# Pinning two engines to program order in a hybrid attention and RWKV-7 layer, with some side work issued in smaller lots

## The chip, the cores and the metric

The kernel runs on one core of one Trainium2 chip. A core has five engines with queues of their own: TensorE (PE, matmuls into PSUM), VectorE (DVE), ScalarE (ACT), GpSimd (POOL) and SyncE (SP, which here issues the transfers). They run side by side and wait for each other by semaphores. The metric is the device time of the core in microseconds (us); lower is better.

## The reference

One layer over 256 frames of width 4096, in float32. A combined projection feeds 16 heads of forgetting attention ("fox", 128 wide), 32 heads of RWKV-7 (64 wide) and a gate; the gated outputs go through an output projection and a layer norm with residual.

```python
proj = jnp.einsum('bsd,dc->bsc', x, w_in)
...
log_f = jax.nn.log_sigmoid(ff.astype(f32) + f_bias.astype(f32))
fox_out = _fox_attention(q, k, v, log_f)   # softmax(q.k/sqrt(Dh) + cumsum(log_f)[t] - cumsum(log_f)[s]), causal
...
rw = rw + (rw_prev - rw) * mu_shift        # token shift by one frame
w_raw = -jax.nn.softplus(-(w0 + jnp.tanh(wd) @ w_up)) - 0.5
decay = jnp.exp(-jnp.exp(w_raw)); a = jax.nn.sigmoid(a0 + ad @ a_up)
...
y = _rwkv7_scan(r, decay, k, v, -kk, kk * a)   # S_t = S_{t-1} diag(decay) + (S_{t-1} a) b^T + v k^T ; y_t = S_t r_t
y = groupnorm_per_head(y) * gn_gain + gn_bias + bonus
h = jnp.concatenate([fox_out, rwkv_out], axis=-1) * jax.nn.silu(z)
out = jnp.einsum('bsc,cd->bsd', h, w_out)
x = layernorm(ALPHA * x + out, ln_gain, ln_bias)
```

(Two calls and the group norm are written in short here.)

## The kernel before

**Weight pieces.** Both projections are long rows of matmuls whose weights stream from memory. A *piece* is two k-tiles by 512 columns, 512 KB: SyncE loads it (L220, four raw buffers), ScalarE casts it to the matmul's format as the high part (L141, four buffers), VectorE subtracts to get the low part (L142, three buffers), and TensorE runs 12 products with 512 columns each: for two k-tiles and two halves of the frames, high by high, high by the input's low part, and low by high (L147, L148, L149; in the output projection L880, L881, L882). There are 624 pieces beside the first block. They are called w{n}_{b}_{q}, with n the pair of heads (0 to 7), b the block of columns within it (0 to 3) and q the piece (0 to 15), then wo{b}_{q} for the output projection. The profile leaves the numbers n and b out, so w_7l is the low part of piece 7 of some block. The first block, with the small columns of the low-rank paths beside it, is loaded in another form (wl, wr). `weights()` keeps three split pieces in hand, so the split of piece q+2 is emitted before the products of piece q.

**Side work.** All else is written as Python generators that stand in `sides`. `slot()` takes one step of each; it is called twice in each piece, so one step is half a piece. `yield from wait(k)` lets k steps pass. The generators are:

- `ahead()`: `lora()` (L313 to L326, transposes and token shift of the low-rank columns, a Tanh), then `prepare(i)` for the 16 column tiles (decays, keys, norms; `front(i)`, L422 to L450, makes decay and rate).
- `chain()`: `forget()` (L337 to L360: the log sigmoid of the forget gate with an Exp and a Ln on ScalarE, a reciprocal L347, a scan L353, and transposes L359), then `rwkv(n)` for the eight pairs: masks (L553 and L561), a triangular inverse (L600, L603), centring of the values (L620 to L627), four chunks of state (L647, L678, L687 and the copies L650, L681, L693), the readout yp (L707, L709), and the group norm: square and gain L714, L716, sums over heads L457, L459 and L462, root L719 to L721, spreading L466, scaling L725 and L726.
- `unload(n, b, ...)`: takes a finished block's tile bk (copied out of PSUM by L918 or L920), transposes it on VectorE (L809), stores and reloads it by way of DRAM (L283: bt, raw), and shifts tokens (L277, L278) or makes silu (L371, L372).
- `fox(i)`: scores (L743, L744), mask, maximum, exponential, reciprocal and scaling (L750 to L754), transposes (L758, copied by L760) and the product with the values (L764, L765).
- `gate()`: silu times output and its split (L380, L383, L384), and a store (hd, reloaded as h for the output projection).

**PSUM.** Blocks accumulate in pairs of tiles from a pool of three (`pp`); the side work has five more (`ps`). So the second accumulator of a block can be written only after L920 has copied the first one of the block before.

**The output projection.** Its blocks run b = 0 and 1 interleaved, then 2 to 7. At the end of block 0 the work pool is closed and `load_tok(0)` and `load_tok(1)` are called: they load the residual and the rows of gain and bias (rr, one buffer, L866 and L867), and split these rows (L869, L871, L872). After each block, `add` (L891, L892) and `gain` (L896, L899, L900) bring it into the residual.

**Order.** The kernel is written with Tile: the program emits instructions, and a scheduler orders each engine's queue by its own model, subject to the data. `tc.keep_in_program_order(...)` fixes an instruction's place among the others so marked on its engine. Before, only a few are marked: the transfers issued through `issue()` (L283), the input's casts, and some transposes and copies; `behind()` holds two other groups behind the latest split:

```python
def behind(first):
    return tc.issue_after(latest[0].ins) if first else nullcontext()
```

Of the kernel before, what the change touches and what calls it, by code (L numbers as in the profile page):

```python
# [14 lines left out]
ALU = mybir.AluOpType  # L15
# [69 lines left out]
def layer(ctx: ExitStack, tc: tile.TileContext, xt, xtok, w_main, w_lora, w_first, muv, w_o, up, par, mulora, fbias, lng, lnb, cst, out):  # L85
    nc = tc.nc
    PS = bass.MemoryType.PSUM
# [36 lines left out]
    nc.vector.memset(warm, 0.0)  # L124
    tc.keep_in_program_order(nc.scalar.activation(warm, warm, AF.Tanh))
# [10 lines left out]
    latest = [None]  # L136

    def split(src, n, name, pool=wpool, tag="", cols=1024):
        hi = pool.tile([P, cols], F32R, tag="wh" + tag, name=name + "h", bufs=4 if pool is wpool else 1)
        lo = pool.tile([P, cols], F32R, tag="wl" + tag, name=name + "l")  # L140
        nc.scalar.copy(hi[:, :n], src[:, :n])  # L141
        latest[0] = nc.vector.tensor_tensor(lo[:, :n], src[:, :n], hi[:, :n].bitcast(F32), ALU.subtract)  # L142
        return hi, lo
# [14 lines left out]
    for n, (k0, k1) in enumerate(pieces):  # L158
        for k in range(k0, k1):
            t = xpool.tile([P, 2, S], F32R, tag=f"x{k}", name=f"x{k}")  # L160
            r = x_raw[n][:, (k - k0) * S : (k - k0 + 1) * S]
            tc.keep_in_program_order(nc.scalar.copy(t[:, 0, :], r))
            nc.vector.tensor_tensor(t[:, 1, :], r, t[:, 0, :].bitcast(F32), ALU.subtract)
# [10 lines left out]
    nc.vector.tensor_scalar(half, prm[:, 0:2, :], 0.5, None, ALU.mult)  # L174
    nkk = const.tile([P, G], F32, name="nkk")
    nc.vector.tensor_scalar(nkk, prm[:, PAR.index("k_k"), :], -1.0, None, ALU.mult)
    omm = const.tile([P, 3, G], F32, name="omm")
    nc.vector.tensor_scalar(omm, prm[:, 7:10, :], -1.0, 1.0, ALU.mult, ALU.add)
    oml = const.tile([LORA, 2], F32, name="oml")
    nc.vector.tensor_scalar(oml, mul, -1.0, 1.0, ALU.mult, ALU.add)  # L180
    ika = PAR.index("k_a")
    hka = const.tile([P, 2, G], F32, name="hka")
    nc.vector.tensor_scalar(hka[:, 0, :], prm[:, ika, :], 0.5, None, ALU.mult)
    nc.vector.tensor_scalar(hka[:, 1, :], prm[:, ika, :], -0.5, 1.0, ALU.mult, ALU.add)
    gneps = const.tile([P, 1], F32, name="gneps")
    nc.vector.memset(gneps, GN_EPS)

    def behind(first):
        return tc.issue_after(latest[0].ins) if first else nullcontext()
# [33 lines left out]
    def fetch():  # L223
        while len(raws) < 3 and stream:
            load()
        if raws:
# [7 lines left out]
            for j in range(2):  # L234
                r = raw[:, j * OB : (j + 1) * OB]
                nc.scalar.copy(hl[j], r)
                nc.vector.tensor_tensor(hl[2 + j], r, hl[j].bitcast(F32), ALU.subtract)
# [38 lines left out]
    def lerp(p, mu, om, dst):  # L276
        nc.scalar.mul(dst, p, om)  # L277
        nc.vector.scalar_tensor_tensor(dst[:, 1:], p[:, : S - 1], mu, dst[:, 1:], ALU.mult, ALU.add)  # L278
# [3 lines left out]
    def issue(out, src):  # L282
        tc.keep_in_program_order(nc.sync.dma_start(out=out, in_=src))  # L283
# [19 lines left out]
    for m in range(2):  # L303
        nc.scalar.copy(lw[:, m, :], acc_l[m][:, :LW])
        nc.scalar.copy(bk_0[:, m, :P], acc_l[m][:, LW:LA])
    ff = []

    def lora():
# [9 lines left out]
        nc.vector.tensor_scalar(u, fft[:NF, :S], fb, None, ALU.add)  # L318
        ff.append(u)
        for j in range(2):  # L320
            t = rp.tile([LORA, S], F32, tag="zt", name=f"lw{j}")
            lerp(lt2[:LORA, j * S : (j + 1) * S], mul[:, j : j + 1], oml[:, j : j + 1], t)
            if j == 0:
                nc.scalar.activation(t, t, AF.Tanh)
            nc.scalar.copy(lr[:, j, 0, :], t)
            nc.vector.tensor_tensor(lr[:, j, 1, :], t, lr[:, j, 0, :].bitcast(F32), ALU.subtract)  # L326
# [4 lines left out]
    def forget():  # L331
# [5 lines left out]
        nc.vector.tensor_scalar(e, u, -1.0, None, ALU.mult)  # L337
        nc.vector.tensor_tensor(e, e, u, ALU.min)
        nc.scalar.activation(e, e, AF.Exp)
        e1 = ft("fe1")  # L340
        nc.vector.tensor_scalar(e1, e, 1.0, None, ALU.add)
        lg = ft("flg")
        nc.scalar.activation(lg, e1, AF.Ln)
        rest = ft("frest")
        nc.vector.tensor_scalar(rest, e1, -1.0, None, ALU.add)
        nc.vector.tensor_tensor(rest, e, rest, ALU.subtract)
        nc.vector.reciprocal(e1, e1)  # L347
        nc.vector.tensor_tensor(rest, rest, e1, ALU.mult)
        nc.vector.tensor_tensor(lg, lg, rest, ALU.add)
        nc.vector.tensor_scalar(u, u, 0.0, None, ALU.min)  # L350
        nc.vector.tensor_tensor(lg, u, lg, ALU.subtract)
        nc.vector.memset(e, 1.0)
        nc.vector.tensor_tensor_scan(rest, e, lg, 0.0, ALU.mult, ALU.add)  # L353
        nc.vector.tensor_scalar(lg, rest, -1.0, None, ALU.mult)
# [5 lines left out]
        nc.vector.tensor_copy(ct, ctp[:, : 2 * NF])  # L360
# [8 lines left out]
    def silu2(z, key):  # L369
        th = t256("zt", key + "t")  # L370
        nc.scalar.activation(th, z, AF.Tanh, scale=0.5)  # L371
        nc.vector.scalar_tensor_tensor(z, th, 1.0, z, ALU.add, ALU.mult)  # L372
        szs[key] = z

    def gate(y, key, k):
# [4 lines left out]
        nc.vector.scalar_tensor_tensor(h, y, 0.5, szs[key], ALU.mult, ALU.mult)  # L380
        pool, tag, bufs = (rp, "hl", 2) if far else (xpool, f"x{k}", 1)
        hl = pool.tile([P, 2, S], F32R, tag=tag, name=f"hl{k}", bufs=bufs)
        nc.scalar.copy(hl[:, 0, :], h)  # L383
        nc.vector.tensor_tensor(hl[:, 1, :], h, hl[:, 0, :].bitcast(F32), ALU.subtract)  # L384
# [34 lines left out]
    def front(i):  # L419
        upt = ups[i]  # L420
        uph = rp.tile([LORA, 2, P], F32R, tag="uph", name=f"uph{i}")
        nc.scalar.copy(flat(uph), flat(upt))  # L422
        upl = rp.tile([LORA, 2, P], F32R, tag="upl", name=f"upl{i}")
        nc.vector.tensor_tensor(flat(upl), flat(upt), flat(uph).bitcast(F32), ALU.subtract)
# [9 lines left out]
        nc.scalar.activation(tw, lp[:, :S], AF.Tanh, scale=0.5, bias=half[:, 0, i : i + 1])  # L434
        ta = rt(f"ta{i}")
        nc.scalar.activation(ta, lp[:, S:], AF.Tanh, scale=0.5, bias=half[:, 1, i : i + 1])
        yield
        nc.vector.tensor_scalar(tw, tw, -0.5 * DECAY, -0.5 * DECAY, ALU.mult, ALU.add)
        L = rt(f"L{i}")
        nc.vector.tensor_tensor_scan(L, cs[:, C_SCAN : C_SCAN + S], tw, 0.0, ALU.mult, ALU.add)  # L440
        eL = rp.tile([P, NCH, C + 1], F32, tag="eL", name=f"eL{i}")
        nc.gpsimd.memset(eL[:, :, 0:1], 1.0)
        nc.scalar.activation(eL[:, :, 1:], ch(L), AF.Exp)
# [674 lines left out]
```

## Time and profile before

| | |
|---|---|
| median of three runs | 1937.24 us (1934.83 to 1940.58) |
| the profiled execution | 1935.4 us |
| its span in the trace | 1933.6 us |
| granted TensorE clock | 0.999 |
| VectorE busy | 1363.2 us |
| ScalarE busy | 963.5 us, with 18 loads of function tables |
| transfers | 420.04 MB, 217 GB/s on average |

A row of the timeline gives start and duration in us, engine, line, operation, the tiles written and read with their shapes, and in brackets how long the engine had been idle before and what ended that. A row of the waits gives the engine and the line that waited, whom it waited for, and then the total in us, how often, and the longest.

### The profile page before, as it was taken

What the parts mean: (1) busy time and instruction counts of PE and PEld (TensorE: products, weight loads), DVE (VectorE), ACT (ScalarE), POOL (GpSimd) and SP (SyncE); (2) the same over time, 40 slices, a digit from 0 to 9 for tenths busy, and PEclk for the clock granted to TensorE, in tenths of its full rate; (3) what the DMA queues carried; (4) which work ended last, traced back from release to release, by engine and by line L of the source; (5) the groups of instructions that cost most, each with busy time, mean ns of one, the idle gap of its engine ahead of it and who ended that gap; (6) DMA issues with size and microseconds to landing.
All of it is one profiled execution on the core that took longest, in us unless ns stands there. A gap on an engine that the chain in (4) does not pass through costs nothing.

```text
span 1933.6 us, 27829 instructions
## 1 busy us (share of the span) xinstructions
PE 1916.5 (99%) x9897; PEld 1594.4 (82%) x9897; DVE 1363.2 (71%) x2323; ACT 963.5 (50%) x1447; POOL 124.2 (6%) x207
## 2 busy tenths in 40 slices
PE   9999999999999999999999999999999999999998
PEld 9888788788888888888888888888888888888886
DVE  6677768857786778677857795779577856755555
ACT  6554464455545644464456444645464554443332
POOL 0020002000200020002000200020001001000000
PEclk9999999999999999999999999999999999999999
DMA  9577667767686778677867677777777777766564
GB/s 343 152 237 229 200 199 215 223 201 216 206 238 198 214 214 236 195 216 211 233 195 220 211 228 202 217 212 220 215 210 221 238 278 242 251 199 197 186 204 166
DMA packets 269391, 420.04 MB, mean 217 GB/s; under 512 B 142338, under 2 KB 169364, under 8 KB 269252
## 3 DMA queue, kind: packets, MB, share of 16 engines
q1 hardware_dynamic: 268820, 417.58, 70.7%
q8 instruction: 77, 1.26, 0.3%
q10 hardware_dynamic: 432, 0.69, 0.1%
q14 instruction: 62, 0.51, 0.1%
HBM read 388.55 MB, written 29.64 MB: 216 GB/s over the span
## 4 chain that ended last, share of the span: by engine, by line
PE 95%; DVE 3%; DMA 1%; issue 0%; ACT 0%; SPq 0%; DVEq 0%; ACTq 0%
PE acc L147 23%; PE acc L149 23%; PE acc L148 23%; PE oacc L880 6%; PE oacc L881 6%; PE oacc L882 6%; PE gp L536 1%; PE rh L647 1%; PE up L678 1%; PE sp L687 1%; PE accl L149 0%; PE accl L148 0%; PE accl L147 0%; PE yp L709 0%; DVE prod L600 0%; DVE xc L603 0%
## 5 line engine op out<-in xcount | busy, mean ns | idle before, releaser
L603 DVE TENSOR_REDUCE xc<-prod 128x8 f32<-128x16 f32 (+30 forms) x248 | 73.1, 295 | 6.5
L600 DVE TENSOR_TENSOR prod<-Nb,xc 128x8 f32<-128x8 f32 (+30 forms) x248 | 71.4, 288 | 6.5 <-DMA Nb<-nd 0.4
L142 DVE TENSOR_TENSOR w_6l<-w,w_6h 128x1024 fp32r<-128x1024 f32 x31 | 37.9, 1222 | 37.5 <-ACT w_6h L141 25.4
L142 DVE TENSOR_TENSOR w_5l<-w,w_5h 128x1024 fp32r<-128x1024 f32 x31 | 41.3, 1333 | 29.5 <-PE acc L149 23.2
L142 DVE TENSOR_TENSOR w_12l<-w,w_12h 128x1024 fp32r<-128x1024 f32 x31 | 38.0, 1227 | 33.5 <-issue 13.8
L740 POOL TENSOR_SCALAR_AFFINE_SELECT nb<-nb 128x128 f32<-128x128 f32 x32 | 15.8, 498 | 705.2 <-DMA nb<-ncd 514.0
L141 ACT CAST w_12h<-w 128x1024 fp32r<-128x1024 f32 x31 | 32.5, 1050 | 48.4 <-DMA w<-in_w_main_dram 19.1
L142 DVE TENSOR_TENSOR w_10l<-w,w_10h 128x1024 fp32r<-128x1024 f32 x31 | 37.9, 1223 | 24.0 <-issue 17.9
L142 DVE TENSOR_TENSOR w_7l<-w,w_7h 128x1024 fp32r<-128x1024 f32 x31 | 37.9, 1222 | 22.1 <-PE acc L149 15.3
L141 ACT CAST w_13h<-w 128x1024 fp32r<-128x1024 f32 x31 | 32.5, 1049 | 40.7 <-PE acc L148 29.0
L141 ACT CAST w_5h<-w 128x1024 fp32r<-128x1024 f32 x31 | 32.6, 1051 | 40.1 <-PE acc L148 37.1
L142 DVE TENSOR_TENSOR w_11l<-w,w_11h 128x1024 fp32r<-128x1024 f32 x31 | 37.9, 1221 | 19.7 <-PE acc L149 19.7
L142 DVE TENSOR_TENSOR w_8l<-w,w_8h 128x1024 fp32r<-128x1024 f32 x31 | 37.8, 1219 | 19.7 <-PE acc L149 15.4
L149 PE MATMUL acc<-w_7l,x 128*128 128x512 f32 x124 | 47.7, 394 | 3.9 <-DVE w_7l L142 3.8
L147 PE MATMUL acc<-w_8h,x 128*128 128x512 f32 x124 | 50.8, 410 | 0.0
L147 PE MATMUL acc<-w_7h,x 128*128 128x512 f32 x124 | 49.9, 403 | 0.2 <-ACT w_7h L141 0.2
L142 DVE TENSOR_TENSOR w_13l<-w,w_13h 128x1024 fp32r<-128x1024 f32 x31 | 37.9, 1222 | 17.2 <-issue 8.3
L147 PE MATMUL acc<-w_3h,x 128*128 128x512 f32 x124 | 49.9, 403 | 0.0
L147 PE MATMUL acc<-w_5h,x 128*128 128x512 f32 x124 | 49.8, 402 | 0.0
L147 PE MATMUL acc<-w_11h,x 128*128 128x512 f32 x124 | 49.8, 402 | 0.0
L147 PE MATMUL acc<-w_15h,x 128*128 128x512 f32 x124 | 49.6, 400 | 0.0
L147 PE MATMUL acc<-w_9h,x 128*128 128x512 f32 x124 | 49.2, 397 | 0.0
(813 smaller groups left out, 6518.7 us busy)
## 6 DMA issues: line engine op xcount, KB each, us to landing
w<-in_w_main_dram SPq DMA_DIRECT2D x496, 512.0 KB, 3.9
wo<-in_w_o_dram SPq DMA_DIRECT2D x128, 512.0 KB, 4.4
bt<-bk SPq DMA_DIRECT2D x88, 128.0 KB, 4.2
Nb<-nd SPq DMA_DIRECT2D x16, 512.0 KB, 4.7
hd<-hl SPq DMA_DIRECT2D x29, 256.0 KB, 3.5
h<-hd SPq DMA_DIRECT2D x29, 256.0 KB, 6.5
wr<-in_w_first_dram SPq DMA_DIRECT2D x15, 384.0 KB, 6.4
lr<-in_w_lora_dram SPq DMA_DIRECT2D x14, 336.0 KB, 5.2
```

The lines of the kernel that those rows point to most:

```text
L141: nc.scalar.copy(hi[:, :n], src[:, :n])
L142: latest[0] = nc.vector.tensor_tensor(lo[:, :n], src[:, :n], hi[:, :n].bitcast(F32), ALU.subtract)
L147: nc.tensor.matmul(acc[:, :n], xs[k][:, 0, tt], hi[:, o : o + n], start=(k == 0), stop=False)
L148: nc.tensor.matmul(acc[:, :n], xs[k][:, 1, tt], hi[:, o : o + n], start=False, stop=False)
L149: nc.tensor.matmul(acc[:, :n], xs[k][:, 0, tt], lo[:, o : o + n], start=False, stop=(k == KT - 1))
L536: nc.tensor.matmul(o, BK[h, u, c, :], lt[j][h, u, c], start=True, stop=True)
L600: first = nc.vector.tensor_tensor(prod[:, :, :, s + 1 :], nb[:, :, s : s + 1, s + 1 :].to_broadcast([P, 2, NJ, w]), xc[:, :, :, s + 1 :], ...
L603: nc.vector.tensor_reduce(xc[:, :, :, s : s + 1], prod[:, :, :, s:], AX.X, ALU.add)
L647: nc.tensor.matmul(rh[:, u * P : (u + 1) * P], LT[:, u, c, 0:P], flat(SVt[:, u, c]), start=True, stop=True)
L880: nc.tensor.matmul(acc, ht[k][:, 0, tt], hi, start=(k == 0), stop=False)
L881: nc.tensor.matmul(acc, ht[k][:, 1, tt], hi, start=False, stop=False)
L882: nc.tensor.matmul(acc, ht[k][:, 0, tt], lo, start=False, stop=(k == KT - 1))
```

## The change

Every instruction on VectorE and on ScalarE is marked to keep program order (`pin`). `latest`, `behind()` and the import of `nullcontext` go. TensorE, SyncE and GpSimd keep the marks they had. Further `yield`s split lots of side work in two, half a piece apart: after each half of the masks, after each half of the centring (the wait behind it is shorter by two), between the exponentials of the softmax and its scaling (the wait behind it is shorter by one), between the root and the reciprocal of the group norm, after each token shift, and between the two silus.

In the changed program as built, counts of instructions by engine stay the same, and so does the number of table loads; three of those at L371 move to L434 and three to L752.

```diff
+    pin = tc.keep_in_program_order
...
-    latest = [None]
-
     def split(src, n, name, pool=wpool, tag="", cols=1024):
         hi = pool.tile([P, cols], F32R, tag="wh" + tag, name=name + "h", bufs=4 if pool is wpool else 1)
         lo = pool.tile([P, cols], F32R, tag="wl" + tag, name=name + "l")
-        nc.scalar.copy(hi[:, :n], src[:, :n])
-        latest[0] = nc.vector.tensor_tensor(lo[:, :n], src[:, :n], hi[:, :n].bitcast(F32), ALU.subtract)
+        pin(nc.scalar.copy(hi[:, :n], src[:, :n]))
+        pin(nc.vector.tensor_tensor(lo[:, :n], src[:, :n], hi[:, :n].bitcast(F32), ALU.subtract))
         return hi, lo
...
-    def behind(first):
-        return tc.issue_after(latest[0].ins) if first else nullcontext()
...
     def forget():
...
-        nc.vector.tensor_scalar(e, u, -1.0, None, ALU.mult)
-        nc.vector.tensor_tensor(e, e, u, ALU.min)
-        nc.scalar.activation(e, e, AF.Exp)
+        pin(nc.vector.tensor_scalar(e, u, -1.0, None, ALU.mult))
+        pin(nc.vector.tensor_tensor(e, e, u, ALU.min))
+        pin(nc.scalar.activation(e, e, AF.Exp))
...
         for u in range(2):
             for j in range(2):
                 h = HALF[j]
-                nc.vector.tensor_tensor(gb[j][h, u], gv[u][j][h], m(h), ALU.mult)
+                pin(nc.vector.tensor_tensor(gb[j][h, u], gv[u][j][h], m(h), ALU.mult))
...
+            yield
         for u in range(2):
             for j in range(2):
                 o = HALF[1 - j]
-                nc.vector.tensor_tensor(lt[j][o, u], ..., ALU.mult)
+                pin(nc.vector.tensor_tensor(lt[j][o, u], ..., ALU.mult))
+            yield
...
                 for a in range(2):
-                    with behind(not n):
-                        nc.vector.scalar_tensor_tensor(SV[j][o, :, 2 * a + c, :], ...)
-            tc.keep_in_program_order(nc.scalar.copy(UV[j][o], SV[j][o]))
+                    pin(nc.vector.scalar_tensor_tensor(SV[j][o, :, 2 * a + c, :], ...))
+            pin(nc.scalar.copy(UV[j][o], SV[j][o]))
             nc.gpsimd.memset(SV[j][HALF[j], :, 0, :], 0.0)
-        yield from wait(W["d2"] - 1)
+            yield
+        yield from wait(W["d2"] - 3)
...
-        nc.vector.tensor_tensor(hr[:, 0, :], hr[:, 0, :], hr[:, 1, :], ALU.add)
-        nc.scalar.activation(hr[:, 0, :], hr[:, 0, :], AF.Sqrt, scale=1.0 / HD, bias=gneps)
-        nc.vector.reciprocal(hr[:, 1, :], hr[:, 0, :])
+        pin(nc.vector.tensor_tensor(hr[:, 0, :], hr[:, 0, :], hr[:, 1, :], ALU.add))
+        pin(nc.scalar.activation(hr[:, 0, :], hr[:, 0, :], AF.Sqrt, scale=1.0 / HD, bias=gneps))
+        yield
+        pin(nc.vector.reciprocal(hr[:, 1, :], hr[:, 0, :]))
         spread(flat(sd), hr[:, 1, :])
...
-        for m, blk in enumerate((slice(0, 1), slice(1, 3))):
-            with behind(i < 2):
-                nc.vector.scalar_tensor_tensor(lg[:, blk, :], spv[:, blk, :], ..., nb[:, blk, :], ALU.add, ALU.add)
-            nc.vector.tensor_reduce(st[:, m : m + 1], lg[:, blk, :], AX.XY, ALU.max, negate=True)
-            nc.scalar.activation(lg[:, blk, :], lg[:, blk, :], AF.Exp, ...)
-            nc.vector.reciprocal(st[:, 4 + m : 5 + m], st[:, 2 + m : 3 + m])
-            nc.vector.tensor_scalar(lg[:, blk, :], lg[:, blk, :], st[:, 4 + m : 5 + m], None, ALU.mult)
-        yield from wait(W["fp"])
+        blocks = list(enumerate((slice(0, 1), slice(1, 3))))
+        for m, blk in blocks:
+            pin(nc.vector.scalar_tensor_tensor(lg[:, blk, :], spv[:, blk, :], ..., nb[:, blk, :], ALU.add, ALU.add))
+            pin(nc.vector.tensor_reduce(st[:, m : m + 1], lg[:, blk, :], AX.XY, ALU.max, negate=True))
+            pin(nc.scalar.activation(lg[:, blk, :], lg[:, blk, :], AF.Exp, ...))
+        yield
+        for m, blk in blocks:
+            pin(nc.vector.reciprocal(st[:, 4 + m : 5 + m], st[:, 2 + m : 3 + m]))
+            pin(nc.vector.tensor_scalar(lg[:, blk, :], lg[:, blk, :], st[:, 4 + m : 5 + m], None, ALU.mult))
+        yield from wait(W["fp"] - 1)
...
                     rk[i, j] = shifted(raw[:, j, :], j, i)
+                    yield
...
         silu2(zf, f"f{i}")
+        yield
         silu2(zr, f"r{i}")
...
         rh = rpool.tile([6, OB], F32R, tag="rh", name=f"rh{b}")
-        nc.scalar.copy(rh, rr)
+        pin(nc.scalar.copy(rh, rr))
...
-        nc.vector.tensor_tensor(res[m][:, o], res[m][:, o], lgain[b], ALU.mult)
+        pin(nc.vector.tensor_tensor(res[m][:, o], res[m][:, o], lgain[b], ALU.mult))
         if m and b < HALVED:
             gx[b] = [rpool.tile([P, OB], F32R, name=f"g{'hl'[j]}{b}") for j in range(2)]
-            nc.scalar.copy(gx[b][0], res[m][:, o])
-            nc.vector.tensor_tensor(gx[b][1], res[m][:, o], gx[b][0].bitcast(F32), ALU.subtract)
+            pin(nc.scalar.copy(gx[b][0], res[m][:, o]))
+            pin(nc.vector.tensor_tensor(gx[b][1], res[m][:, o], gx[b][0].bitcast(F32), ALU.subtract))
```

Every other instruction of the two engines, here and in the parts left out, is wrapped in `pin(...)` in the same way and is otherwise unchanged.

More of the change, by code (lines that the diff above doesn't have):

```diff
@@ L1 @@
 import math
-from contextlib import ExitStack, nullcontext
+from contextlib import ExitStack
 import numpy as np
@@ L317, in lora @@
         u = rp.tile([NF, S], F32, tag="t", name="fu", bufs=5)
-        nc.vector.tensor_scalar(u, fft[:NF, :S], fb, None, ALU.add)
+        pin(nc.vector.tensor_scalar(u, fft[:NF, :S], fb, None, ALU.add))
         ff.append(u)
@@ L766, in fox @@
         o = t256("fq", f"fo{i}")
-        nc.scalar.copy(o, op[:, :S])
+        pin(nc.scalar.copy(o, op[:, :S]))
         while f"f{i}" not in szs or 2 * i >= FAR and not closed:
@@ L836, in unload @@
                 for t in range(2):
-                    nc.scalar.copy(pair[t], tr[:, t * S : (t + 1) * S])
+                    pin(nc.scalar.copy(pair[t], tr[:, t * S : (t + 1) * S]))
                 yield
@@ L845, in unload @@
             yield from wait(LAND - 1)
[L846 removed]
+        pin(nc.scalar.mul(fq, fq, FOX_SCALE))
         side(fox(i, fq, fk, vt))
@@ L933, in layer @@
                 for m in range(2):
-                    nc.scalar.copy(vt[:, m, :], acc[m][:, 2 * P :])
+                    pin(nc.scalar.copy(vt[:, m, :], acc[m][:, 2 * P :]))
             if b != 1:
@@ L1021, in row @@
         t = rpool.tile([P, P], F32R, name="l" + name)
-        nc.scalar.copy(t, zp[:, :P])
+        pin(nc.scalar.copy(t, zp[:, :P]))
         return t
@@ L1032, in finish @@
         nc.tensor.matmul(wp, l, rows[:, o], start=True, stop=True)
-        nc.vector.scalar_tensor_tensor(res[m][:, o], res[m][:, o], rss[m], wp, ALU.mult, ALU.add)
+        pin(nc.vector.scalar_tensor_tensor(res[m][:, o], res[m][:, o], rss[m], wp, ALU.mult, ALU.add))
     z0, _, last = moments(0)
```

233 lines of the change are left out of this document (116 added, 117 removed).

## The prediction

> **What bounds the kernel now.** I read the page's busy shares first, then the waits of TensorE, then the timelines of the stretches where the printed order of instructions, built from the changed program, differs most.
>
> ```profile
> span 1933.6 us, 27829 instructions
> ...
> PE 1916.5 (99%) x9897; PEld 1594.4 (82%) x9897; DVE 1363.2 (71%) x2323; ACT 963.5 (50%) x1447; POOL 124.2 (6%) x207
> ```
>
> TensorE is busy for 99% of the span, VectorE and ScalarE for 71% and 50%. So TensorE's queue sets the end, and the other two matter where they hand a split weight piece over late.
>
> ```profile
> PE acc L149 <- DVE w_7l L142: 3.8, 2, 3.4
> PE zp L1020 <- DVE zd L1008: 1.4, 1, 1.4
> PE warmup L108 <- POOL idle L105: 1.3, 1, 1.3
> ```
>
> These are the three largest of twelve rows. All twelve come to 10.1 us: that is everything a change on VectorE and ScalarE can win, and the second (the tail) and the third (the start) don't depend on it. The first row has the one long wait, of 3.44 us:
>
> ```profile
> 379.96 0.50 PE L149 MATMUL acc<-w_7l,x 128*128 128x512 f32 x1 [3.44 <-DVE w_7l L142]
> ...
> 380.00:383.00 3.00, 3.00 (x13) 2.46 (x14) 2.00 (x4) 1.59 (x3) 0.00 (x0) 1.00 0.65 199
> ```
>
> TensorE stood still until VectorE delivered the low part of a piece, and then ran on at a granted clock of 1.00, 13 products in 3.00 us or 0.23 us each. A piece has 12 products, so 2.73 us. Two pieces stand ready behind the one in use, so a hold-up of up to about 5.4 us on VectorE or ScalarE costs nothing, and each microsecond beyond it is a microsecond of the span.
>
> **The change part by part.** The instructions are the same ones; no product, cast or transfer is added. Three things move. The pins fix both engines' queues to the order in which the program emits work. The extra yields put parts of a lot half a piece later. And what the scheduler had pulled forward or spread out (the constants of the output, the forget gate, the group norm's end) falls back to where it is emitted. What that costs is read along the changed order, each instruction with its duration in the rows. For each signal between engines I add 0.05 and for each small product 0.1 (estimates from the gaps in the timelines).
>
> *First weight block.*
>
> ```profile
> 69.07 0.33 PE L149 MATMUL acc<-wr16l,x 128*128 128x384 f32 x1
> 69.25 0.39 PE L147 MATMUL acc<-w_0h,x 128*128 128x512 f32 x1
> ...
> 70.22 0.48 ACT L918 COPY bk<-acc 128x384 f32<-128x384 f32 x1
> ...
> 71.98 1.05 ACT L141 CAST w_4h<-w 128x1024 fp32r<-128x1024 f32 x1 [0.98 <-PE acc L148]
> ...
> 1655.11 1.22 DVE L142 TENSOR_TENSOR wo_0l<-wo,wo_0h 128x1024 fp32r<-128x1024 f32 x1
> ```
>
> Before, the three first casts of block w0_1 were made long ahead, and its first product starts 0.18 us after the last of the block before it. In the changed order both L918 copies stand ahead of the cast of w0_1_0, and the second waits for the last product, which ends at 69.40. Then 0.48 of copy and 1.05 of cast give 70.9, and 1.22 of subtraction gives 72.2. TensorE can do four products from the high part first, so the low part is due at 70.2: 2.0 us late. Six small transposes run inside the gap; I take 1.5.
>
> *Forget gate and low-rank path.*
>
> ```profile
> 74.23 0.47 DVE L318 TENSOR_SCALAR fu<-fft,fb 16x256 f32<-16x256 f32 x1 [0.80 <-PE fft L316]
> ...
> 80.32 1.73 DVE L347 RECIPROCAL fe<-fe 16x256 f32<-16x256 f32 x1
> ...
> 86.39 0.15 DVE L360 COPY ct<-ctp 128x32 f32<-128x32 f32 x1
> ...
> L809 DVE STREAM_TRANSPOSE bk<-bk x44: 690/702/716, 69.0 to 1419.3; 128x512 f32<-128x512 f32 x44
> ...
> 77.94 1.28 ACT L343 ACT_TABLE_LOAD   x1
> ```
>
> From L318 to L360 VectorE has 20 instructions for this work, and before, three splits were placed among them. Now all 20 and the two L809 transposes stand between the splits of w0_1_3 and w0_1_4. Their durations come to 10.2 us, of which 1.73 is L347 and 1.40 L809, and the round trips to ScalarE (L324, L325, L339) to 1.9. After w0_1_3's low part at 76.0 that gives 88.2, and 89.4 for the low part of w0_1_4. TensorE has done pieces 0 to 3 and the small products (some 1.8) by 84.0 and wants the low part at 84.9: 4.5 us late, or 4.9 if the transposes of L359, which wait for the scan, take longer. I take 4.7. ScalarE's Ln load (77.94) falls in the shade of L347. The next piece waits behind the exponentials of L443 to L448, which wait for L440: low part 94.2, due at 92.1, so 2.0.
>
> ```profile
> bt<-bk SPq DMA_DIRECT2D x88, 128.0 KB, 4.2
> ...
> raw<-bt SPq DMA_DIRECT2D x16, 256.0 KB, 4.7
> ...
> 72.61 3.64 SPq L283 DMA_DIRECT2D bt<-bk  x4
> ```
>
> The turned tile bt0_0 is late as well: transposed by 88.1 instead of near 70, four issues of 3.64 in all, 4.2 to land, then 4.7 for raw0 give 100.6. L277 of raw0 now stands on ScalarE ahead of the cast of w0_1_8, which so comes 2.0 to 2.6 late, and pieces 9 and 10 follow with 2.3 us of preparation each: 2.5 to 3.7. I take 2.5, as the stores may overlap their landing. The start costs 1.5 + 4.7 + 2.0 + 2.5 = 10.7; bounds 7 and 13.
>
> *Ends of the head pairs.*
>
> ```profile
> 1404.65 0.69 DVE L459 TENSOR_REDUCE hry<-hqy 128x16 f32<-128x512 f32 x1
> ...
> 1406.39 0.18 DVE L719 TENSOR_TENSOR hry<-hry 128x16 f32<-128x16 f32 x1 [1.05 <-POOL hry L462]
> ...
> 1407.23 0.71 DVE L466 STREAM_TRANSPOSE post<-hry 128x512 f32<-128x512 f32 x1
> ...
> 1411.17 0.42 DVE L380 SCALAR_TENSOR_TENSOR h<-post,zr 128x256 f32<-128x256 f32 x1
> ...
> 1416.03 0.74 DVE L750 SCALAR_TENSOR_TENSOR lg<-fsp,ct,nb 128x128 f32<-128x128 f32 x2
> ...
> 1416.68 0.60 DVE L751 TENSOR_REDUCE fst<-lg 128x1 f32<-128x128 f32 x2
> ...
> 1409.12 1.28 ACT L371 ACT_TABLE_LOAD   x1
> ...
> 1410.42 0.42 ACT L371 ACTIVATE f13t<-zf 128x256 f32<-128x256 f32 x1
> ...
> 1416.42 0.59 ACT L920 COPY bk<-acc 128x512 f32<-128x512 f32 x1 [0.91 <-PE acc L149]
> ...
> 1416.99 0.40 ACT L752 ACTIVATE lg<-lg,fst 128x128 f32<-128x128 f32 x1
> ```
>
> Before, the group norm of a pair (L714 to L726), the gate (L380, L383), the softmax (L750 to L754) and the copies L920 are spread over seven pieces. In the changed order they meet around w6_1_0 and w6_1_1. Take zero at the start of w6_0_14 on TensorE. The last product of yp5 is done at 1.5, L714 and L716 by 2.9, the cast of w6_1_0 by 3.9, its low part by 5.2. L719, ready since 4.7, comes behind that, so 5.4; the root ends at 5.7, a load for Exp of 1.28 at 7.0, the two exponentials (start to start 0.9 with their sums) at 8.0. Only then is w6_1_1 cast: 9.0, low part 10.3. Behind it on VectorE stand L721, L466, four short softmax steps (0.9), L725, L726 and L380: 13.2. L383 waits for that and L920 stands behind L383: 14.2. L920 frees the accumulator in which TensorE wants to do the second halves of w6_1_0 and w6_1_1, at 10.1 (pieces 14 and 15 at 2.73, two halves at 1.36, small products 1.95). So 4.1 us are lost, and the same order stands at w5_1 and w7_1. At w1_1 it is the softmax behind the last states of the pair, 3.9; at w4_1, where L720 stands after the split, 1.95; at w2_1 and w3_1 1.0 and 0.45. Sum 3 × 4.1 + 3.9 + 1.95 + 1.0 + 0.45 = 19.6. The lower bound is 6, if the scores come a piece sooner than I place them, the upper 24.
>
> [...]
>
> *Start of the output's later blocks.*
>
> ```profile
> 1648.05 0.47 DVE L871 TENSOR_SCALAR rt<-rh,cs 6x512 f32<-6x512 f32 x1
> 1648.56 0.74 DVE L872 SCALAR_TENSOR_TENSOR rows<-rr,cs,rt 6x512 fp32r<-6x512 f32 x1
> ...
> 1651.43 1.36 DVE L891 SCALAR_TENSOR_TENSOR res<-res,oacc 128x512 f32<-128x512 f32 x2 [0.81 <-PE oacc L882]
> ...
> 1653.91 1.27 DVE L896 TENSOR_TENSOR res<-res,lg 128x512 f32<-128x512 f32 x2
> ...
> 1655.56 0.61 ACT L899 CAST gh<-res 128x512 fp32r<-128x512 f32 x1
> ...
> 1657.35 0.39 PE L880 MATMUL oacc<-wo_0h,h 128*128 128x512 f32 x1
> ...
> L867 SPq DMA_DIRECT2D rr<-in_lnb_dram x8: 261/270/308, 1616.1 to 1682.3; - x8
> ...
> L869 ACT CAST rh<-rr x8: 610/614/619, 1620.2 to 1685.5; 6x512 fp32r<-6x512 f32 x8
> ```
>
> L869 to L872 were spread over the blocks before, for four tiles by then. Pinned, they run where the program emits them, after the split of wo1_15, which ends at 1650.5. L973, L871 and L872 of tile 0 end at 1651.95. There is one rr buffer, so the two loads for tile 1 start only now. From L867 to L869 the last tile took 3.2 and the first 4.1, an upper bound; I take 2.5, which gives 1654.5. L869, L871, L872: 1656.5. L891 and L892 (2.48 here, 2.7 in the new alternation), L896 1.27: 1660.5. L899, 0.61, waits for it and stands ahead of the cast of wo2_0: high part 1662.1, low part 1663.4, wanted at 1657.8: 5.6. Then L899 of the second tile stands in the same way ahead of wo2_2: 2.4, and at the next two blocks 0.45 each. Sum 8.9; bounds 6 and 11.
>
> *Small change on the other side.* TensorE goes over to small products and back some ten times more than before, at 0.1 to 0.2 each: 1.5. The waits on w_7l go (3.8), since masks are half a piece apart; with the small ones for other pieces −4.8. The yields between silu, shifts, centring and masks cost nothing: their readers are a piece or more away. If that cover is gone, it is half a piece, 1.4, for each.
>
> **Sum.** 10.7 + 19.6 + 8.9 + 1.5 − 4.8 = 35.9 on the profiled execution's 1935.4, which is 1.8 above its span and 1.8 below the median shown: 1971.3.
>
> **Rivals.** *The pair ends are hidden.* If two ready pieces suffice there, because the scores and yp5 are done earlier, 19.6 goes: 1951.7. For it: before, VectorE idles in this stretch. Against it: L383 and L920 are single queues of waits, whatever VectorE's share.
>
> *All hidden, faster.* If the chains between two splits stay below 5.4 us everywhere, only the −4.8 and 1.5 are left: 1932.1. It is decided at the forget gate, where 12.1 us stand between two splits; that is against it.
>
> *The change does not bind.* If the engines' order hardly mattered, the time stays at 1935.4. The printed order is another one in every block, which speaks against it.
>
> *A cold clock after long waits.* Six of the waits exceed the longest seen, 3.44, after which the clock was 1.00.
>
> ```profile
> 4.80 0.48 PE L148 MATMUL accl<-wl0h,x 128*128 128x336 f32 x1
> 5.08 0.48 PE L147 MATMUL accl<-wl0h,x 128*128 128x336 f32 x1
> ```
>
> At the start, products of 336 columns are 0.28 apart, about twice 0.23 × 336 / 512. If each of the six waits brings that back for 3 to 5 us, it loses 1.5 to 2.5 each time, some 12 in all: 1983. [...]
>
> **How the numbers follow.** My forecast has 0.55, with a range of its own of 1957 to 1981; hidden pair ends 0.18, cold clock 0.12, no change 0.06, all hidden 0.07, 0.02 for others. The bounds of the terms (19 and 48 before the small ones) reach 1951 to 1981. From 1944 to 1984 leaves out the two cases at or below 1936 and the top of the cold clock, together under 0.2. About 0.3% (5.8 us) is what a measurement of this kernel tells from no change, so faster 0.07, same 0.06, slower 0.87.
>
> **What would show it.** TensorE's waits should name w0_1_4's low part (4 to 5 us), the L920 copies or L758 near w5_1, w6_1, w7_1 (about 4 each) and wo2_0 (5 to 6), while the 3.8 on w_7l is gone; VectorE's and ScalarE's busy time must stay as they are. TensorE's waits below 20 us in all, or waits that name a DMA, prove me wrong.

## The result and the profile after

The changed kernel takes 2052.77 us (median of four, 2050.42 to 2056.75), the kernel before 1937.14 us (median of four): a ratio of 1.060 with a 95% interval of 1.057 to 1.062. The forecast was slower, at 1971 us; the loss is 3.2 times what I worked out. In the rows of the changed kernel the lines are those of its own file: the cast of a weight piece is L140 there, its subtraction L141, the products L146 to L148, h and the gate's cast L376 and L379, the copies out of PSUM L923.

The page of the changed kernel, its span and the busy time of each engine:

```profile
span 2055.0 us, 27764 instructions
PE 1980.0 (96%) x9897; PEld 1601.9 (78%) x9897; DVE 1398.0 (68%) x2323; ACT 944.7 (46%) x1447; POOL 121.2 (6%) x207
```

and the granted clock of its core (time from first to last instruction, mean clock):

```profile
core 0: 2055.0 us, clock 0.986
```

The span grew by 121.4 us. VectorE and ScalarE are busy as long as before within 3% (1398.0 and 944.7 us), as they must be. TensorE's busy time grew by 63.5 us though its products are the same, and the clock fell from 0.999 to 0.986. So two things have to be found: waits, and slow products. TensorE's waits in the changed kernel (engine and line that waited, whom for, total, times, longest):

```profile
PE acc L146 <- ACT w_1h L140: 9.6, 10, 2.4
PE acc L146 <- ACT bk L923: 7.4, 5, 2.0
PE oacc L883 <- ACT wo_0h L140: 5.6, 2, 4.5
PE acc L146 <- ACT w_0h L140: 5.4, 4, 1.5
PE fpt L759 <- DVE fst L754: 4.1, 8, 0.9
PE ctp L355 <- DVE frest L349: 3.9, 1, 3.9
PE acc L148 <- DVE w_1l L141: 3.9, 7, 0.8
```

All rows of this view come to 65.9 us in 86 waits, against 10.1 before. No single wait is long; the longest is 4.5 us, and the one of 3.4 us on w_7l is gone. The places I named are there (ctp 3.9, wo_0h 5.6, bk 7.4, and 4.1 on L759, which was L758 before), but they are a third of the sum.

The slow products show in the view of stretches, here of 3.4 us each. The columns are the stretch, its length, busy time and count of PE, PEld, DVE, ACT and POOL, the clock, and DMA. The changed kernel around w1_1_0:

```profile
274.00:277.40 3.40, 1.20 (x4) 0.72 (x5) 1.73 (x6) 1.53 (x3) 0.00 (x0) 1.00 0.00 0
277.50:280.90 3.40, 3.40 (x17) 2.59 (x16) 1.03 (x3) 2.93 (x6) 0.00 (x0) 0.50 0.50 159
280.90:284.30 3.40, 3.40 (x12) 2.21 (x12) 2.25 (x4) 0.46 (x1) 0.00 (x0) 0.50 0.48 152
284.40:287.80 3.40, 3.40 (x66) 3.07 (x63) 1.19 (x3) 1.20 (x3) 0.40 (x2) 1.00 0.65 179
```

TensorE waited 2.2 and 0.5 us in the first stretch, and for the next 6.8 us it ran at half clock (0.50). The changed kernel has eleven such spells before its tail, six of 3.41 us and five of 6.83, together 54.6 us. Taken against the products in them, they cost 25.5 us. In the kernel before, at a mean clock of 0.999, the trace has none before its tail.

Between the starts of the same products, the growth splits so (sums over all product starts of the two traces, each product set against its usual spacing before):

| part | us |
|---|---|
| waits that the profile names (73 more than before) | 55.9 |
| lag at these waits and just behind them | 20.0 |
| half clock | 25.5 |
| other spacing of main products, at full clock | 12.1 |
| small products and changes over to and from them | 7.8 |

The second part belongs to the waits. A wait is counted only after the modelled end of the product ahead (0.39 after its start, against 0.23 of spacing), and the first spacing after a wait is about 0.34, as at 379.96 and 380.31 in the trace before. That is some 0.3 us on top of each wait. Of the fourth part some 5 us are hold-ups of 0.15 to 0.32 us, too short for the view of waits; the rest I can't place.

### The profile page after: what moved, and what is told of

Same layout as the page of the kernel before. It is cut to its first block, busy times and chain, and to the rows that moved or that the text cites. A ratio compares the mean times of both kernels' runs of the same rounds, so it can differ in the third digit from the quotient of the medians.

```text
span 2055.0 us, 27764 instructions
## 1 busy us (share of the span) xinstructions
PE 1980.0 (96%) x9897; PEld 1601.9 (78%) x9897; DVE 1398.0 (68%) x2323; ACT 944.7 (46%) x1447; POOL 121.2 (6%) x207
## 5 line engine op out<-in xcount | busy, mean ns | idle before, releaser
L146 PE MATMUL acc<-w_0h,x 128*128 128x512 f32 x124 | 54.4, 439 | 13.5 <-ACT bk L923 7.4
L141 DVE TENSOR_TENSOR w_2l<-w,w_2h 128x1024 fp32r<-128x1024 f32 x31 | 37.9, 1224 | 39.3 <-ACT w_2h L140 39.3
L146 PE MATMUL acc<-w_1h,x 128*128 128x512 f32 x124 | 52.2, 421 | 9.6 <-ACT w_1h L140 9.6
L141 DVE TENSOR_TENSOR w_0l<-w,w_0h 128x1024 fp32r<-128x1024 f32 x31 | 37.9, 1221 | 31.7 <-ACT w_0h L140 24.2
L141 DVE TENSOR_TENSOR w_1l<-w,w_1h 128x1024 fp32r<-128x1024 f32 x31 | 37.9, 1223 | 29.7 <-ACT w_1h L140 21.7
L379 ACT CAST hl<-h 128x256 fp32r<-128x256 f32 x32 | 13.0, 406 | 97.5 <-DVE h L376 94.8
L141 DVE TENSOR_TENSOR w_7l<-w,w_7h 128x1024 fp32r<-128x1024 f32 x31 | 38.1, 1230 | 26.9 <-ACT w_7h L140 22.1
L141 DVE TENSOR_TENSOR w_8l<-w,w_8h 128x1024 fp32r<-128x1024 f32 x31 | 37.9, 1223 | 27.0 <-ACT w_8h L140 23.2
L148 PE MATMUL acc<-w_1l,x 128*128 128x512 f32 x124 | 51.7, 417 | 3.9 <-DVE w_1l L141 3.9
L141 DVE TENSOR_TENSOR w_12l<-w,w_12h 128x1024 fp32r<-128x1024 f32 x31 | 37.8, 1220 | 25.2 <-ACT w_12h L140 23.6
L141 DVE TENSOR_TENSOR w_11l<-w,w_11h 128x1024 fp32r<-128x1024 f32 x31 | 38.2, 1233 | 24.2 <-ACT w_11h L140 16.1
L148 PE MATMUL acc<-w_0l,x 128*128 128x512 f32 x124 | 53.3, 431 | 1.1 <-DVE w_0l L141 1.0
L141 DVE TENSOR_TENSOR w_15l<-w,w_15h 128x1024 fp32r<-128x1024 f32 x31 | 37.9, 1223 | 24.0 <-ACT w_15h L140 12.6
L141 DVE TENSOR_TENSOR w_5l<-w,w_5h 128x1024 fp32r<-128x1024 f32 x31 | 46.1, 1487 | 10.2 <-ACT w_5h L140 6.6
L146 PE MATMUL acc<-w_4h,x 128*128 128x512 f32 x124 | 50.1, 404 | 2.6 <-ACT w_4h L140 2.6
L146 PE MATMUL acc<-w_8h,x 128*128 128x512 f32 x124 | 51.0, 411 | 1.5 <-ACT w_8h L140 1.5
L140 ACT CAST w_7h<-w 128x1024 fp32r<-128x1024 f32 x31 | 32.5, 1048 | 43.2 <-DMA w<-in_w_main_dram 35.1
L147 PE MATMUL acc<-w_0h,x 128*128 128x512 f32 x124 | 52.3, 422 | 0.0
L141 DVE TENSOR_TENSOR w_14l<-w,w_14h 128x1024 fp32r<-128x1024 f32 x31 | 37.8, 1219 | 20.5 <-ACT w_14h L140 11.0
```

The costliest lines, as they stand in the source:

```text
L140: pin(nc.scalar.copy(hi[:, :n], src[:, :n]))
L141: pin(nc.vector.tensor_tensor(lo[:, :n], src[:, :n], hi[:, :n].bitcast(F32), ALU.subtract))
L146: nc.tensor.matmul(acc[:, :n], xs[k][:, 0, tt], hi[:, o : o + n], start=(k == 0), stop=False)
L147: nc.tensor.matmul(acc[:, :n], xs[k][:, 1, tt], hi[:, o : o + n], start=False, stop=False)
L148: nc.tensor.matmul(acc[:, :n], xs[k][:, 0, tt], lo[:, o : o + n], start=False, stop=(k == KT - 1))
L379: pin(nc.scalar.copy(hl[:, 0, :], h))
```

## The experiments

Each run is of the kernel named, on the chip, with its own profile; the time is a single run unless an interval stands with it. The kernel before, run beside them, took 1935 to 1941 us. In the diffs, `pa` marks ScalarE's and `pd` VectorE's instructions; where one of them is `free`, the marks and holds of before are left on that engine. The rows of each run carry the line numbers of its own file.

**Smaller lots alone.**

```diff
-    pin(nc.vector. ...)        # and pin(nc.scalar. ...)
+    nc.vector. ...             # marks and behind() as before; all new yields stay
```

> The smaller lots alone: the added yields, with the marks for program order and the holds behind the latest split as before the change. Theory A (the loss comes from the fixed order: a cast of a weight piece stands on ScalarE behind side work that waits for VectorE, and the other way round): 1930 to 1940 us, and TensorE's wait of 3.8 us on w_7l gone. Rival B (the loss comes from the lots that now come half a piece later, so that readers wait): 1970 us or more. Rival C (VectorE's order alone does it): as A.

Measured: 1976.53 us, ratio 1.020 (1.018 to 1.022). Theory A fails: the wait on w_7l grew instead of going. The time lies in Rival B's range, but its mechanism doesn't show. The largest row of the waits names one place, in six of the pairs (L159 are the products from the low part, L152 the subtraction):

```profile
PE acc L159 <- DVE w_7l L152: 26.6, 6, 7.1
```

and VectorE's timeline ahead of the longest of them is

```profile
770.32 1.22 DVE L152 TENSOR_TENSOR w_6l<-w,w_6h 128x1024 fp32r<-128x1024 f32 x1
771.46 0.31 DVE L612 TENSOR_REDUCE xc<-prod 128x8 f32<-128x152 f32 x1
...
781.85 0.42 DVE L612 TENSOR_REDUCE xc<-prod 128x8 f32<-128x256 f32 x1
...
784.11 1.21 DVE L152 TENSOR_TENSOR w_7l<-w,w_7h 128x1024 fp32r<-128x1024 f32 x1
```

The scheduler put 12.6 us of the triangular inverse and the centring between the low parts of pieces 6 and 7. The kernel before has such a run of work in one pair only, ahead of its own wait on w_7l. A reader of a late lot is not what waits here (Rival B's mechanism): the order changed. Why the scheduler answered so isn't shown.

**Pins alone, and the pins of one engine.**

> Every VectorE and ScalarE instruction pinned, lots as before the change (no added yield, softmax in one lot). Theory A: 2040 to 2100 us, as much as the change or more, since masks and softmax stand in larger lots ahead of the splits. Rival B: below 1990. Rival C: 2040 to 2100.

> The change with VectorE's marks as before the change and all of ScalarE pinned. Theory A: between, 1960 to 2010 us, since casts still stand behind ScalarE's side work, but VectorE delivers what they wait for early; ScalarE's idle time before the gate's cast hl falls from 94.8 us to under 40. Rival C: 1930 to 1945.

> The change with ScalarE's marks as before the change and all of VectorE pinned. Theory A: between, 1960 to 2010 us. Rival C (VectorE's order alone): 2030 us or more.

Measured: 2063.89, 1998.25 and 1998.84 us. All three lie in Theory A's ranges, and in the second ScalarE's idle time before hl is 32.8 us, below the 40 expected. Rivals B and C fall: without the yields the pins cost 11 us more than with them, and neither engine's order alone brings the loss. The last two runs have the new yields, which by themselves cost 39 us. One engine's pins add 22 to that, the pins of both add 76: most of it comes only when both queues are fixed. (With ScalarE alone pinned, the largest wait is still the one on w_7l, 31.7 us in six.) The yields and the pins aren't additive either (39 and 127 apart, 116 together).

**Weight pieces left to the scheduler.**

```diff
-        pin(nc.scalar.copy(hi[:, :n], src[:, :n]))
-        pin(nc.vector.tensor_tensor(lo[:, :n], src[:, :n], hi[:, :n].bitcast(F32), ALU.subtract))
+        nc.scalar.copy(hi[:, :n], src[:, :n])
+        nc.vector.tensor_tensor(lo[:, :n], src[:, :n], hi[:, :n].bitcast(F32), ALU.subtract)
```

> The change with only the weight pieces' cast and subtraction (split) left to the scheduler; all other VectorE and ScalarE instructions pinned, lots as in the change. Theory A (pieces are late because they stand in the fixed queues behind side work that waits for the other engine): TensorE's waits fall from 67 us to below 35, the time to 1950 to 1995 us. Rival (the side work's own chain is what is late, and TensorE's small products wait for it): 2030 us or more.

Measured: 1965.15 us. 88 of the 116 us come back, with all side work still in fixed order. The half-clock spells before the tail fall from 54.6 to 17.0 us (mean clock 0.995 instead of 0.986), and TensorE's waits from 66 to 20. So the side work's own chain is not what is late. With one of the two freed:

> The change with only the cast of the weight pieces on ScalarE left to the scheduler; their subtraction on VectorE stays pinned. Theory A1 (it is ScalarE's queue: the cast stands behind side casts that wait for VectorE): most of what the run with the whole split free won comes here, 1965 to 1995 us. Theory A2 (both queues share it about evenly): 2000 to 2025 us.

> The change with only the subtraction of the weight pieces on VectorE left to the scheduler; their cast on ScalarE stays pinned. Theory A1: 2035 to 2055 us, as the subtraction has to wait for the cast anyway. Theory A2: 2000 to 2025 us.

Measured: 2013.34 and 2050.76 us. Neither A1 nor A2 fits: ScalarE's place wins 39 us, VectorE's 2, and both together 88. A subtraction can't pass its cast, and a cast that comes early leaves the subtraction behind VectorE's side work. In the run with the cast free, the largest wait is on a subtraction (w_15l, 17.6 us in five).

**Side casts emitted later.** First the gate's alone, then three kinds:

```diff
         pin(nc.vector.scalar_tensor_tensor(h, y, 0.5, szs[key], ALU.mult, ALU.mult))
...
+        yield
         pin(nc.scalar.copy(hl[:, 0, :], h))
...
+        yield
         pin(nc.scalar.copy(lt[1][HALF[1]], lt[0][HALF[1]]))
...
             pin(nc.vector.tensor_reduce(st[:, m : m + 1], lg[:, blk, :], AX.XY, ALU.max, negate=True))
+        yield
+        for m, blk in blocks:
             pin(nc.scalar.activation(lg[:, blk, :], lg[:, blk, :], AF.Exp, ...))
```

> The change with one more yield in gate(), between VectorE's h and ScalarE's cast hl, so that the cast is emitted half a piece after what it waits for. Theory A: ScalarE's idle time before hl falls from 94.8 us to below 40, TensorE's waits on the casts of pieces 1 to 5 fall, 2020 to 2040 us. Rival (the next instruction in the chain takes the place of the one moved): 2048 us or more.

> The change with three kinds of ScalarE instructions emitted half a piece after the VectorE result that they wait for (one more yield each): the gate's cast hl, the copy of lt, the softmax's exponentials. Everything stays pinned, so the queues are as fixed as in the change. Theory A (what harms is a side instruction ahead of the cast that waits for VectorE): ScalarE's idle time before these three, 198 us in the changed kernel, falls below 120, and the time to 2000 to 2032 us. Rival (the wait only passes to the next instruction in the fixed queue): 2036 us or more.

Measured: 2038.38 us for the first, in Theory A's range, but its mechanism doesn't show. ScalarE's idle time ahead of hl fell from 94.8 to 51.0, not below 40, and that ahead of the copy of lt rose from 61.6 to 81.9 and ahead of the exponentials from 41.9 to 64.9: nearly all of it passed on, as the rival has it. TensorE's waits on the casts of pieces 1 to 5 rose from 15.5 to 32.9 us instead of falling. Where these 14 us come from stays open. With all three moved, 2020.19 us, also in Theory A's range; the three idle times come to 136.8 us instead of 198, more than the 120 expected, and the waits on those casts to 7.2. Every mark stayed, so it is what stands ahead of a cast, and not the mark, that costs. That is Theory A, with a smaller step than I gave it.

**Four side casts without a mark.**

> The change with four kinds of ScalarE instructions left to the scheduler, those that wait longest for VectorE in the changed kernel: the gate's cast hl, the copy of lt, the softmax's exponentials and the copies R. Casts of weight pieces and all else stay pinned. Theory A (what harms is what stands ahead of the cast, not the cast's own mark): 1975 to 2015 us, and ScalarE's idle time before hl below 40 us. Rival (the rest of ScalarE's queue blocks as much): 2035 us or more.

Measured: 2057.36 us. It tells nothing of the theory: ScalarE's instructions stand in the same order as in the changed kernel, instruction for instruction. Without a mark, the scheduler put each where it was emitted. The run is a second run of the change.

**The two ends left to the scheduler.**

> The change with the first block's copies, the low-rank path, the forget gate, and load_tok, add and gain of the output left to the scheduler; all else pinned. As worked out in the prediction for these two places (10.7 and 8.9 us, and now with the half-speed spells at 86.4, 1670.1 and 1776.0 us of the changed kernel): 2028 to 2038 us, and these spells gone. If these places cost less than the trace seems to show: 2045 us or more.

Measured: 2039.40 us, 13.4 less than the change. The spells at 86.4, 1670.1 and 1776.0 are gone (mean clock 0.993 instead of 0.986). It lies just above what I expected: the start, to the end of w0_3, still takes 7.2 us more than before, and the output 3.3 more, with a wait of 1.5 us in it.

**A version to beat both.**

```diff
+        latest[0] = pin(nc.vector.tensor_tensor(lo[:, :n], ...))   # VectorE: low parts and the inverse pinned, all else as before, with the new yields
+            first = pin(nc.vector.tensor_tensor(prod[:, :, :, s + 1 :], ...))
+            pin(nc.vector.tensor_reduce(xc[:, :, :, s : s + 1], ...))
```

> The smaller lots with the marks of before, and in addition only the low part of the weight pieces and the steps of the triangular inverse pinned on VectorE. In the run with the smaller lots alone, 11 to 16 us of inverse steps stood ahead of the low part of piece 7 once in each pair. Theory A: these waits go and nothing else comes: 1929 to 1937 us. Rival (the scheduler puts other side work there instead): 1950 us or more.

> The kernel before with only the two yields after the halves of the masks, and no added pin. If the wait of 3.4 us on w_7l near 376 us comes from the masks and nothing else moves: 1931 to 1935 us. If the scheduler answers with another order, as in the run with the smaller lots alone: 1945 us or more.

Measured: 1956.51 us (ratio 1.010, 1.008 to 1.012) and 1963.26 us (1.013, 1.011 to 1.015), both as the rivals had it. The first takes away the waits behind the inverse and gets one of 4.5 us at the output, behind low parts that now keep their place. The second has w_7l waits of 2 to 4.5 us in six pairs. Neither beats the kernel before, and I found no version that does.

**The clock after waits of known length.** Fills of the low part's tile ahead of one subtraction in seven pairs, in the kernel before:

```diff
+DELAY = {f"w{n}_2_8": k for n, k in zip(range(1, 8), (5, 5, 6, 6, 7, 8, 8))}   # second run: (1, 1, 2, 2, 2, 3, 3)
...
+        for _ in range(DELAY.get(name, 0)):
+            nc.vector.memset(lo.bitcast(F32), 0.0)
         nc.scalar.copy(hi[:, :n], src[:, :n])
```

> The kernel before, with 5, 5, 6, 6, 7, 8 and 8 extra fills of the low part's tile ahead of the subtraction of piece 8 of block 2 of pairs 1 to 7; the fills are overwritten, so nothing is left out. At about 1 us a fill, TensorE should wait some 1, 1, 2, 2, 3, 4 and 4 us there. [...] Sum 1956 to 1968 us.

> As the run with the delays, with 1, 1, 2, 2, 2, 3 and 3 fills. From its waits (4.6 us for 5 fills, 0.9 us a fill) TensorE should wait about 1.2, 1.2, 2.0, 2.0, 2.0, 3.0 and 3.0 us at piece 8. [...]

Measured: 1998.29 and 1941.47 us. The waits came out longer than planned in the first (4.6 to 8.2 us, a fill takes 0.91 and starts only when the buffer is free) and shorter in the second (up to 1.75). All seven places of the first have a half-clock spell, none of the second's (mean clock 0.985 and 0.997); no wait there came out between 1.75 and 4.6. The place that tells more is one I hadn't touched: the wait of 3.44 us on w_7l, the same in the kernel before and in the second run. Before, TensorE's 3.4-us stretches around it read

```profile
375.00:378.40 3.40, 1.53 (x7) 0.94 (x5) 3.26 (x12) 0.00 (x0) 0.00 (x0) 1.00 0.05 22
378.40:381.80 3.40, 1.83 (x8) 1.52 (x9) 2.95 (x5) 0.39 (x2) 0.00 (x0) 1.00 0.22 45
```

and in the second run with delays, where the wait ends 0.57 us later, the stretch with the wait and the one after it read

```profile
378.30:381.70 3.40, 1.17 (x5) 0.98 (x6) 3.35 (x7) 0.00 (x0) 0.00 (x0) 1.00 0.13 13
381.80:385.20 3.40, 3.40 (x9) 2.64 (x8) 1.79 (x3) 3.23 (x4) 0.00 (x0) 0.50 0.81 284
```

with the products in TensorE's timeline

```profile
380.53 0.50 PE L152 MATMUL acc<-w_7l,x 128*128 128x512 f32 x1 [3.44 <-DVE w_7l L145]
...
381.34 0.40 PE L152 MATMUL acc<-w_7l,x 128*128 128x512 f32 x1
...
382.26 0.63 PE L152 MATMUL acc<-w_7l,x 128*128 128x512 f32 x1
382.68 0.63 PE L150 MATMUL acc<-w_7h,x 128*128 128x512 f32 x1
```

The same wait is followed by half clock in one run (0.50, with 0.43 between products from 381.83 on) and not in the other (1.00 up to 385.20, with 0.23 between products). So its length alone doesn't decide; what does isn't shown. The block with it (w1_3) is 1.6 us longer than before.

## Why the prediction was wrong

The starts of the blocks' and pieces' first products in the two traces give where the span grew, in us. "Waits" are the named waits with their lag, "small" the small products and the changes over to them; what is left is other spacing of main products.

| stretch | grew | waits | half clock | small | prediction |
|---|---|---|---|---|---|
| start, to the end of w0_3 | 10.4 | 8.3 | 2.8 | −0.3 | 10.7 |
| b = 0 blocks, pieces 0 to 13 | 8.4 | 11.2 | 10.0 | −11.7 | 0 |
| pieces 14, 15 of b = 0 and 0 to 2 of b = 1 | 40.1 | 20.5 | 9.4 | 9.7 | 19.6 |
| b = 1 blocks, pieces 3 to 15 | 28.2 | 16.7 | 0 | 6.5 | 0 |
| b = 2 blocks | 8.6 | 5.0 | 0 | 2.4 | 0 |
| b = 3 blocks | 15.4 | 10.0 | 0 | −0.4 | −3.8 |
| output projection | 10.1 | 4.4 | 3.3 | 1.5 | 8.9 |

**What held.** The direction, and most of the places worked out along the changed order. At the start, w0_1_0 comes 1.8 us later (1.5 worked out), and the waits at L355 and on the cast of w0_1_4 come to 4.6 (4.7); the output has 4.5 on the cast of wo2_0 (5.6). The waits are 8.3 and 4.4 in these two rows, and that the sums come so near 10.7 and 8.9 is in part luck: the half clock stands in for smaller waits of mine that didn't come. At the ends of the pairs the waits, 20.5, agree with the 19.6 in sum. Near w5_1, w6_1 and w7_1 they come to about 3.3 each before their lag, but only 1.7 of it is a copy out of PSUM (L923); the rest is mostly the cast and the subtraction of piece 1. The wait on w_7l went, and its block (w1_3) is 3.7 us shorter, but not for the reason I gave, the masks half a piece apart: in the run with those two yields alone, TensorE waits on w_7l in six pairs.

**The step that failed** is the cover: "a hold-up of up to about 5.4 us on VectorE or ScalarE costs nothing", with the three stretches "where the printed order of instructions ... differs most" as the only ones worked out. The rows of the pairs outside their ends, put at nothing but the −3.8, are the others: 42.9 us of waits and 10.0 of half clock. Nor is "each microsecond beyond it ... a microsecond of the span": a wait brings 0.3 more, and behind some the clock was 0.50 (25.5 us in all). I had measured each engine's own load against the two pieces in hand. But the two queues wait for each other. Before, what ended VectorE's idle time ahead of a subtraction was mostly TensorE giving a buffer back, the sign of a full reserve (244 us of 396 in all, ScalarE 81). The three largest rows of VectorE's waits in the kernel before:

```profile
DVE w_6l L142 <- ACT w_6h L141: 25.4, 8, 4.0
DVE w_5l L142 <- PE acc L149: 23.2, 15, 2.0
DVE w_11l L142 <- PE acc L149: 19.7, 17, 1.5
```

In the changed kernel it is mostly ScalarE (263 us of 460, TensorE 187). The same view there:

```profile
DVE w_2l L141 <- ACT w_2h L140: 39.3, 24, 3.0
...
DVE w_12l L141 <- ACT w_12h L140: 23.6, 13, 2.6
DVE w_8l L141 <- ACT w_8h L140: 23.2, 16, 2.2
```

ScalarE in turn waits for VectorE, ahead of side casts. ScalarE's largest waits in the changed kernel, of which the first two were 10.7 and 10.0 us before:

```profile
ACT hl L379 <- DVE h L376: 94.8, 31, 4.7
ACT lt L496 <- DVE lt L495: 61.6, 16, 5.0
ACT R L648 <- DVE R L648: 60.8, 32, 4.4
ACT lg L751 <- DVE fst L750: 41.9, 26, 4.1
```

One turn of it, in block w4_1. ScalarE's timeline, then VectorE's, then TensorE's, all of the changed kernel:

```profile
902.40 1.05 ACT L140 CAST w_4h<-w 128x1024 fp32r<-128x1024 f32 x1
906.99 0.41 ACT L379 CAST hl<-h 128x256 fp32r<-128x256 f32 x1 [3.54 <-DVE h L376]
907.31 0.37 ACT L768 COPY fo<-fop 128x256 f32<-128x256 f32 x1
908.42 0.40 ACT L379 CAST hl<-h 128x256 fp32r<-128x256 f32 x1 [0.75 <-DVE h L376]
908.73 1.04 ACT L140 CAST w_5h<-w 128x1024 fp32r<-128x1024 f32 x1
```

```profile
903.30 1.30 DVE L810 STREAM_TRANSPOSE bk<-bk 128x512 f32<-128x512 f32 x2
904.52 1.18 DVE L141 TENSOR_TENSOR w_4l<-w,w_4h 128x1024 fp32r<-128x1024 f32 x1
905.63 0.41 DVE L724 TENSOR_TENSOR post<-post 128x256 f32<-128x256 f32 x1
906.07 0.43 DVE L725 TENSOR_TENSOR post<-post,bon 128x256 f32<-128x256 f32 x1
906.53 0.43 DVE L376 SCALAR_TENSOR_TENSOR h<-post,zr 128x256 f32<-128x256 f32 x1
907.43 0.43 DVE L380 TENSOR_TENSOR hl<-h,hl 128x256 fp32r<-128x256 f32 x1 [0.47 <-ACT hl L379]
907.96 0.43 DVE L376 SCALAR_TENSOR_TENSOR h<-fo,zf 128x256 f32<-128x256 f32 x1
...
909.80 1.23 DVE L141 TENSOR_TENSOR w_5l<-w,w_5h 128x1024 fp32r<-128x1024 f32 x1 [0.52 <-ACT w_5h L140]
```

```profile
909.83 0.50 PE L146 MATMUL acc<-w_5h,x 128*128 128x512 f32 x1 [1.22 <-ACT w_5h L140]
```

After the cast of w_4 (902.40) ScalarE has the next weight piece's cast to do, but two gate casts and a copy stand ahead of it. The first waits 3.54 us for VectorE, which does two transposes, w_4's subtraction, two scaling steps and h. Then VectorE waits for the cast to do hl, and ScalarE again for the next h. The cast of w_5 starts at 908.73, 6.3 us after that of w_4, with ScalarE busy for only 2.2 us of them. The pieces cost 2.73 us on TensorE, so its reserve shrinks by 3.6 in this one turn. VectorE was busy for 5.3 of the 6.3 us: its own side work is most of the chain, and the handing to and fro adds the rest. That the pieces' places in both queues cost the time is shown by the run with the split free (88 us back, and VectorE's idle time ahead of subtractions again ended mostly by TensorE, 302 us against ScalarE's 82), and the run with three side casts later agrees. How much of the loss is mutual waiting, and how much side work that merely stands ahead, isn't shown apart.

**The half clock.** It was my rival at 0.12 and 12 us, and came at 25.5, beside the other losses and not alone. I set it against the one long wait of the trace before, after which the clock was 1.00, and took six waits over 3.44 us as its condition. The second run with delays has a clock of 0.50 behind a wait of the same 3.44 us, and the changed kernel has it behind waits of 2.2 and 0.5 us in one stretch (277.50 to 284.30). No run shows the 3 to 5 us for each of six waits from which I worked out the 12; in the changed kernel there are six spells of 3.41 us and five of 6.83.

Two smaller terms were off as well. Small products and the changes over to them, put at 1.5, grew by 7.8. The yields, which I costed at nothing, weren't nothing either way: under the pins they win 11 us.

## What to carry to other kernels

When two engines whose queues keep a fixed order hand work to each other, a ready-made reserve is not to be set against each engine's own load but against the chain through both queues: for each piece, add up what stands ahead of its cast on one engine and what those instructions wait for on the other. What ends the idle time of the producers is a hint at how the reserve stands: while they wait for buffers from the consumer it is full. It is no more than a hint: with the cast alone free it looks as in the kernel before (245 us ended by TensorE, 64 by ScalarE), at 2013.34 us, with low parts behind VectorE's side work. And an edit to a program that a scheduler orders is a new order everywhere; look at the order that was built before costing the lot that was meant.

## What the runs showed of the hardware

In the changed kernel the granted clock is 0.50 in eleven spells before the tail, six of 3.41 us and five of 6.83, and its mean over the span is 0.986. At 0.50, products of 512 columns start 0.43 apart (281.39, 281.81 and 282.24); at 1.00 they start 0.23 apart (371.83, 372.06 and 372.29 in the kernel before). Behind waits of 2.2 and 0.5 us the changed kernel has 6.8 us at 0.50, from 277.51 on. Behind the wait of 3.44 us on w_7l the clock was 1.00 in the kernel before (379.96 to 385.20) and 0.50 in the second run with delays (381.80 to 385.20). So half clock followed on a wait of 2.2 us with one of 0.5 behind it, and needn't follow on one of 3.44. What decides it isn't shown.
